# Low parts of the down projection's weights by an accumulating DMA in place of a VectorE subtraction

## The chip, the cores and the metric

The kernel runs on one core of one Trainium2 chip. The metric is the device time of one launch in microseconds (us); less is better. Several launches are timed and the median is compared. One further launch was recorded by the hardware profiler, and every row below comes from that one.

## The reference

Two decoder layers over 512 tokens of width 1024, all in float32. Each layer is RMSNorm, one combined projection, three attention branches, gates, an output projection and a residual add; then RMSNorm, a SwiGLU feed-forward part and a residual add. What matters here is the last line of each layer:

```python
h = rmsnorm(x, ln_ffn_g[l])
x = x + (jax.nn.silu(h @ w_ffn_gate[l]) * (h @ w_ffn_up[l])) @ w_ffn_down[l]
```

`w_ffn_down[l]` is 2816 by 1024. After the second layer one more RMSNorm ends the computation.

## The kernel before

**Precision by three products.** TensorE multiplies in the reduced format `float32r`. So each operand is held as two tiles, a high part (the value rounded to `float32r`) and a low part (the value less its high part), and each product is made of three matmuls into the same PSUM bank: high by high, high by low, low by high (lines 370 to 372). For a weight, the high part is a copy by ScalarE (`_hi`, line 235) and the low part is a subtraction by VectorE (`_lo`, line 243).

**Units.** Weights are loaded in units, each one tile of 128 by 1024 floats (512 KB) of the pool `wides`, which has 36 buffers (`NWIDE`). Feed-forward hidden values, norm gains and temporaries live in the same pool. Every unit has three tiles in turn: the raw load (issued on SP's queue, `_dma`), the high part and the low part. When `_lo` is written, the raw tile is given up; when the unit's matmuls are written, the high and the low part are given up (`done`).

**The down projection.** It is two jobs per layer, one for each half of the 1024 output columns (`j_dn`, lines 1429 and 1430). Each has 11 units of two 128-row blocks of the weight, so 22 units per layer and 44 in all. A unit is used by 2 blocks x 4 token blocks x 3 = 24 matmuls of 512 columns, and in each triple the second matmul is the first one that reads the low part. The second half takes its last four units in one group of eight blocks. The products' other operand, the hidden values, is split by `ffsplit` (line 1309), also one cast by ScalarE and one subtraction by VectorE for each two blocks; 4 of the 11 are written during the feed-forward stage, the others during the first half.

**What sets the order.** The order in which instructions are written is the order of each engine's queue; engines wait for one another through semaphores only. Before each token block of a unit, `ahead` (line 272) writes further loads, high parts and low parts, as far ahead as the three numbers of `look` say, in columns: `LEAN = (3072, 1024, 1024)` in the down projection means loads up to three units ahead of the current one, high parts one unit ahead, low parts one unit ahead, and at most one high and one low part per call. The feed-forward stage writes the down projection's first units near its own end: its last seven slots (one product of 12 matmuls of 256 columns each) are P1, P7, P6, P4, P5, P2, P3, and with four slots left (at P4) and two left (at P2) it calls `ahead` (line 1300), there with `NEAR`. The first of these two calls writes the high and the low part of unit 0, the second the high part of unit 1. At the end of the first half, each token block's result is added to the residual by VectorE and its sum of squares is taken by ScalarE (`residual_evac`, and `final_evac` in the second layer), in those engines' queues. From the last group of the second half, `look` is `FAR`.

In the attention part, a planner (`weave`) orders pieces of work by a modelled clock (`Clock.note`), which keeps a free time for each engine and one for the DMAs. In the down projection the order is fixed by the code above.

Of the kernel before, what the change touches and what calls it, by code (L numbers as in the profile page):

```python
# [11 lines left out]
AF = mybir.ActivationFunctionType  # L12
ALU = mybir.AluOpType
# [22 lines left out]
NEAR = (3072, 1536, 1024)  # L36
WIDE = (4096, 2048, 2048)
FAR = (6144, 4096, 4096)
LEAN = (3072, 1024, 1024)

OFF_QA, OFF_KA, OFF_VA = 0, 512, 1024
OFF_QB, OFF_KB, OFF_VB = 1536, 2048, 2560
# [125 lines left out]
class Kernel:  # L168
# [74 lines left out]
    def _lo(self, i):  # L243
        if i in self.plain:
            return
        t, cols = self.raw.pop(i)
        l = self.wide(F32R)
        self.nc.vector.tensor_tensor(l[:, :cols], t[:, :cols], self.hi[i][:, :cols], op=ALU.subtract)
        self.lo[i] = l

    def load_ahead(self, n):
# [370 lines left out]
def layer(K, l, plan, state, strip, C):  # L622
# [810 lines left out]
    def drain(jobs):  # L1433
        for _ in K.dense(jobs):
            pass

    def run():
# [62 lines left out]
        else:  # L1500
            state["g"] = K.load_g("ln_mix_g", l + 1)
        K.look = LEAN
        drain(j_dn[:1])
# [40 lines left out]
```

## Time and profile before

| | us |
|---|---|
| median of 3 launches | 1838.68 (1838.28 to 1839.81) |
| the profiled launch | 1839.35 |
| its span in the trace | 1837.6 |
| TensorE (PE) busy | 1814.9 (99%) |
| VectorE (DVE) busy | 1112.1 (61%) |
| ScalarE (ACT) busy | 883.1 (48%) |
| GpSimd (POOL) busy | 251.0 (14%) |

The granted TensorE clock was 0.997 of full speed over the span. Times in the trace count from the span's start. PE is a matmul, PEld the load of its stationary operand. A name such as `w` stands for all tiles of a pool whose names begin so (`w` is the pool of 128 by 1024 tiles, `s` that of 128 by 512 tiles, `d` and `a` are PSUM banks). All work is recorded at line 158, a helper's, so operations are told apart by tile, shape and time. A matmul's shown duration overlaps the next one's, so the pace of matmuls is read from starts, or from a long merged row divided by its count. Some records of instructions are missing from the trace.

### The profile page before, as it was taken

To read this page: it belongs to the slowest core of one execution; us is meant where nothing else is said; L and a number is where in the kernel's file an instruction comes from. 1 tells how busy PE (TensorE), PEld (TensorE's weight loads), DVE (VectorE), ACT (ScalarE), POOL (GpSimd) and SP (SyncE) were. 2 spreads that over 40 slices of the span, in tenths; PEclk is the share of its full clock that TensorE was granted. 3 is DMA by queue.
4 is the path that set the end of the run, shared out by engine and by line. 5 is a ranking of instruction groups with operands and counts; after the bars stand their busy time and mean duration, and the time that the engine had idled before them with its cause. 6 is when DMAs were issued, how large, how long until landed. Compare 5 with 4: busy or idle time off the path is not lost.

```text
span 1837.6 us, 27149 instructions
## 1 busy us (share of the span) xinstructions
PE 1814.9 (99%) x10588; PEld 1619.2 (88%) x10588; DVE 1112.1 (61%) x1832; ACT 883.1 (48%) x1701; POOL 251.0 (14%) x437
## 2 busy tenths in 40 slices
PE   7999999999999999999999999999999999999998
PEld 5999888888889999998889998888888899999886
DVE  4566556566456888773345655566664578788631
ACT  4555655554334555552235655555443355545531
POOL 3314312121000000000002252122210000000001
PEclk9999999999999999999999999999999999999999
DMA  7322122223330323242332121132252322233331
GB/s 278 117 89 72 55 72 87 100 81 131 104 138 27 112 93 107 101 149 90 134 126 95 58 69 55 60 104 86 69 178 80 115 69 93 93 115 104 126 103 46
DMA packets 63280, 183.15 MB, mean 100 GB/s; under 512 B 9296, under 2 KB 10768, under 8 KB 63152
## 3 DMA queue, kind: packets, MB, share of 16 engines
q1 hardware_dynamic: 57456, 172.84, 28.3%
q0 software_dynamic: 3824, 4.91, 0.9%
q10 hardware_dynamic: 1872, 3.67, 0.6%
q8 instruction: 83, 1.36, 0.3%
q14 instruction: 45, 0.37, 0.1%
HBM read 177.15 MB, written 8.16 MB: 101 GB/s over the span
## 4 chain that ended last, share of the span: by engine, by line
PE 94%; DVE 2%; ACT 2%; POOL 1%; issue 0%; DMA 0%; POOLq 0%; ACTq 0%
PE d L158 74%; PE a L158 21%; DVE w L158 1%; ACT w L158 1%; POOL s L158 1%; DVE s L158 0%; ACT junk L158 0%; DMA s<-in_c_onehot 0%; POOL w L158 0%; POOL m L158 0%; DVE f_A L158 0%; DVE f_S L158 0%; ACT f_A L158 0%; ACT s L158 0%; DVE h L158 0%
## 5 line engine op out<-in xcount | busy, mean ns | idle before, releaser
L158 PE MATMUL d<-w,w 128*128 128x512 f32 (+2 forms) x3888 | 748.6, 346 | 1.3 <-ACT s L158 0.9
L158 DVE TENSOR_TENSOR w<-w,w 128x1024 fp32r<-128x1024 f32 (+6 forms) x594 | 598.2, 1030 | 190.2 <-ACT w L158 161.6
L158 PEld LDWEIGHTS d<-w,w 128*128 128x128 f32 x3888 | 631.7, 190 | 83.2 <-ACT s L158 1.3
L158 PE MATMUL d<-h,w 128*128 128x512 f32 x1920 | 459.9, 392 | 0.0
L158 ACT CAST w<-w 128x1024 fp32r<-128x1024 f32 (+3 forms) x454 | 399.4, 921 | 96.2 <-PE d L158 46.9
L158 PEld LDWEIGHTS d<-h,w 128*128 128x128 f32 x1920 | 356.0, 188 | 71.4
L158 PE MATMUL d<-w,h 128*128 128x512 f32 (+2 forms) x960 | 199.0, 356 | 3.5 <-DVE h L158 1.8
L158 PEld LDWEIGHTS d<-w,h 128*128 128x128 f32 x960 | 165.1, 190 | 21.2 <-DVE h L158 2.5
L158 ACT ACTIVATE w<-w,m 128x128 f32<-128x128 f32 x192 | 107.0, 558 | 119.1 <-DVE m L158 117.8
L158 POOL TENSOR_SCALAR m<-m 128x1 f32<-128x1 f32 (+1 forms) x44 | 18.4, 419 | 1063.6 <-ACT junk L158 1063.2
L158 PE MATMUL a<-w,w 128*128 128x256 f32 (+7 forms) x912 | 157.9, 310 | 0.0
L158 PEld LDWEIGHTS a<-w,w 128*128 128x128 f32 (+1 forms) x912 | 138.3, 189 | 11.5
L158 PE MATMUL a<-f_A,w 128*128 128x256 f32 x1104 | 147.1, 283 | 0.0
L158 POOL TENSOR_SCALAR w<-w,m 128x128 f32<-128x128 f32 (+3 forms) x160 | 94.5, 608 | 352.4 <-DVE m L158 216.5
L158 PEld LDWEIGHTS a<-f_A,w 128*128 128x128 f32 x1104 | 138.7, 192 | 0.0
L158 DVE TENSOR_TENSOR w<-a,w 128x512 fp32r<-128x512 f32 (+2 forms) x162 | 90.3, 593 | 75.2 <-ACT w L158 74.7
L158 ACT CAST w<-a 128x512 fp32r<-128x512 f32 (+2 forms) x146 | 70.5, 533 | 72.5 <-PE a L158 71.8
L158 ACT ACTIVATE junk<-s 128x512 f32<-128x512 f32 (+1 forms) x40 | 23.6, 589 | 155.0 <-DVE s L158 155.0
L158 ACT COPY s<-d 128x256 f32<-128x256 f32 (+2 forms) x104 | 40.2, 391 | 108.1 <-PE d L158 107.4
L158 POOL TENSOR_SCALAR w<-w 64x512 fp32r<-64x512 f32 (+1 forms) x96 | 69.2, 728 | 125.8 <-issue 87.4
L158 PE MATMUL a<-ident,w 128*128 128x128 f32 x616 | 83.5, 275 | 2.6 <-DVE s L158 2.3
L158 DVE TENSOR_TENSOR s<-d,s 128x512 f32<-128x512 f32 x32 | 22.0, 688 | 105.4 <-PE d L158 105.4
(79 smaller groups left out, 1216.3 us busy)
## 6 DMA issues: line engine op xcount, KB each, us to landing
w<-in_weights SPq DMA_DIRECT2D x246, 512.0 KB, 3.6
w<-in_weights SPq DMA_DIRECT2D x50, 256.0 KB, 2.7
w<-in_weights SPq DMA_DIRECT2D x28, 384.0 KB, 4.3
s<-u_rep SPq DMA_DIRECT2D x24, 256.0 KB, 3.8
w<-in_weights SPq DMA_DIRECT2D x8, 288.0 KB, 3.1
w<-in_x SPq DMA_DIRECT2D x8, 256.0 KB, 7.2
s<-in_x SPq DMA_DIRECT2D x8, 256.0 KB, 5.7
x_dram<-s ACTq DMA_DIRECT2D x8, 256.0 KB, 4.2
```

What stands on the lines that cost most here:

```text
L158: return f(*args, **kw)
```

## The change

For units of the down projection's weight alone, the low part is no longer raw tile less high part on VectorE. ScalarE writes the negated high part into the low part's tile, and then a DMA issued by GpSimd adds the raw tile to it in place. The look-ahead of the down projection also changes: loads up to four units ahead in place of three, high parts three in place of one, low parts two in place of one. The calls of `ahead` at the end of the feed-forward stage are not changed.

```diff
-LEAN = (3072, 1024, 1024)
+LEAN = (4096, 3072, 2048)
...
         l = self.wide(F32R)
-        self.nc.vector.tensor_tensor(l[:, :cols], t[:, :cols], self.hi[i][:, :cols], op=ALU.subtract)
+        if self.units[i][0][0] == "w_ffn_down":
+            self.nc.scalar.activation(l[:, :cols], self.hi[i][:, :cols], AF.Copy, scale=-1.0)
+            self.nc.gpsimd.dma_start(l[:, :cols], t[:, :cols], accum_op=ALU.add)
+        else:
+            self.nc.vector.tensor_tensor(l[:, :cols], t[:, :cols], self.hi[i][:, :cols], op=ALU.subtract)
         self.lo[i] = l
```

## Rows read from the trace of the kernel before

**Rows 1.** The page's first block: busy us, share of the span, instructions.
```profile
PE 1814.9 (99%) x10588; PEld 1619.2 (88%) x10588; DVE 1112.1 (61%) x1832; ACT 883.1 (48%) x1701; POOL 251.0 (14%) x437
```

**Rows 2.** The page's chain that ended last, shares of the span by engine.
```profile
PE 94%; DVE 2%; ACT 2%; POOL 1%; issue 0%; DMA 0%; POOLq 0%; ACTq 0%
```

**Rows 3.** PE's waits, whole span: for whom, us in total, times, longest.
```profile
PE a L158 <- DMA s<-in_c_onehot: 7.9, 1, 7.9
PE a L158 <- DVE s L158: 2.3, 2, 2.0
PE d L158 <- DVE w L158: 2.0, 5, 0.5
PE d L158 <- DVE h L158: 1.8, 1, 1.8
...
PE a L158 <- DVE w L158: 0.3, 1, 0.3
```

**Rows 4.** Timeline, first layer's seam: start, us, instructions merged, [idle before <-releaser].
```profile
797.01 4.84 ACT L158 CAST w<-w 128x1024 fp32r<-128x1024 f32 x5
...
797.99 1.60 PE L158 MATMUL d<-w,w 128*128 128x256 f32 x12
798.10 2.36 DVE L158 TENSOR_TENSOR w<-w,w 128x1024 fp32r<-128x1024 f32 x2 [0.16 <-ACT w L158]
...
800.86 29.35 PE L158 MATMUL d<-w,w 128*128 128x256 f32 x134
```

**Rows 5.** Timeline of ACT alone, 798.1 to 799 us.
```profile
797.96 2.00 ACT L158 CAST w<-w 128x1024 fp32r<-128x1024 f32 x2
```

**Rows 6.** Timeline, matmuls from the first half's end on, first layer.
```profile
859.75 51.62 PE L158 MATMUL d<-w,w 128*128 128x512 f32 x227
```

**Rows 7.** Timeline of ACT, second layer's seam.
```profile
1699.90 0.84 ACT L158 ACTIVATE w<-w 128x768 f32<-128x768 f32 x1
...
1704.21 5.98 ACT L158 CAST w<-w 128x1024 fp32r<-128x1024 f32 x6
```

**Rows 8.** Timeline of PE, second layer's seam.
```profile
1708.06 67.22 PE L158 MATMUL d<-w,w 128*128 128x256 f32 x301
```

**Rows 9.** Timeline of POOL at the kernel's start: DMAs that GpSimd issued.
```profile
30.79 0.60 POOL L158 DMA_DIRECT2D cstrip<-in_c_strip  x1
```

**Rows 10.** DMA issues on the page: queue, count, KB each, median us from issue to landing.
```profile
w<-in_weights SPq DMA_DIRECT2D x246, 512.0 KB, 3.6
w<-in_weights SPq DMA_DIRECT2D x50, 256.0 KB, 2.7
```

**Rows 11.** DMA issues within 796 to 808 us.
```profile
w<-in_weights SPq DMA_DIRECT2D x6, 512.0 KB, 5.4
```

**Rows 12.** DMA issues within 829 to 858 us.
```profile
w<-in_weights SPq DMA_DIRECT2D x5, 512.0 KB, 3.4
```

**Rows 13.** DMA issues, whole span: small and queued ones of GpSimd.
```profile
cstrip<-in_c_strip POOLq DMA_DIRECT2D x1, 256.0 KB, 17.6
...
u_dram<-s POOLq DMA_DIRECT2D x2, 15.0 KB, 1.7
```

**Rows 14.** Stretches: PE, PEld, DVE, ACT, POOL busy (count), PEclk, DMA share, GB/s.
```profile
800.00:803.00 3.00, 3.00 (x24) 2.88 (x23) 2.73 (x5) 2.44 (x3) 0.00 (x0) 1.00 0.98 345
```

**Rows 15.** Timeline of ACT within the first half, first layer.
```profile
840.45 1.05 ACT L158 CAST w<-w 128x1024 fp32r<-128x1024 f32 x1 [4.16 <-PE d L158]
```

**Rows 16.** Timeline, end of the first half, first layer.
```profile
862.44 0.69 DVE L158 TENSOR_TENSOR s<-d,s 128x512 f32<-128x512 f32 x1 [0.67 <-PE d L158]
...
863.85 2.94 ACT L158 CAST w<-w 128x1024 fp32r<-128x1024 f32 x3
864.92 7.16 DVE L158 TENSOR_TENSOR w<-w,w 128x1024 fp32r<-128x1024 f32 x6 [1.79 <-ACT w L158]
...
907.50 0.30 POOL L158 TENSOR_SCALAR m<-m 128x1 f32<-128x1 f32 x1 [329.20 <-ACT junk L158]
```

**Rows 17.** Timeline, end of the first half, second layer.
```profile
1775.70 6.64 PE L158 MATMUL d<-w,w 128*128 128x512 f32 x28 [0.42 <-DVE w L158]
```

## The prediction

> **What bounds the kernel now.** I read the page's busy block first, then the chain, then PE's waits, then the timeline of the stretches in which the changed tiles are made. The busy block shows PE at 99% of the span and DVE at 61% [rows 1]; the chain that ended last is 94% PE and 2% DVE [rows 2]. So a faster DVE is worth only what PE waits for it. The list of PE's waits says how much that is: all its waits on DVE, of every kind, are 2.3 + 2.0 + 1.8 + 0.3 = 6.4 us in the whole launch, and the largest wait, 7.9 us, is for a DMA at the start [rows 3]. In the down projection PE runs without a break, but for one wait: 0.42 us for DVE in the second layer [rows 17]. The question is therefore what the new way of making a low part delays, more than what it frees.
>
> **The pace and the deadlines.** 227 matmuls of 512 columns take 51.62 us [rows 6], 0.227 us each, so a unit of 24 takes 5.46 us. In the first layer the last three products of the feed-forward stage start at 797.99 (P5), 1.435 later (P2) and at 800.86 (P3) [rows 4]; P3 ends at 802.30, and the down projection starts. Unit 0's low part is read by the second matmul, at 802.30 + 0.23 = 802.53. Unit u's is due at 802.53 + 5.46 u. In the second layer P3 starts at 1708.06 [rows 8], so all is 907.2 us later; the cast that starts at 797.01 has its like at 1704.21 [rows 7], also 907.2 later. One working serves both.
>
> **Removed.** 44 subtractions by DVE. Two of them stand in rows 4, the first one unit 0's: 2.36 us for two. All are hidden beside PE except in the place of rows 17, where unit 12's low part, written after four residual adds, comes 0.42 us late. With low parts written two units ahead, unit 12's is written ahead of those adds: gain 0.4 us, once. More than that PE can't give back here, since it waits for nothing else in the stage.
>
> **Added on ACT.** 44 negations of 128 by 1024. The trace has no such instruction; a scaled copy costs ACT what a cast does in the nearest shape, 0.84 us for 128 by 768 [rows 7], and the cast of 128 by 1024 takes 1.05 [rows 15], of which starts follow every 0.97 (4.84 / 5) [rows 4]. I take 1.05. Between 1.0 and 1.2 nothing changes: ACT then has three such instructions in a unit of 5.46 us in the first half, and two in the second.
>
> **Added on POOL and the DMA engines.** 44 DMAs. POOL has nothing else to do: its next instruction after the feed-forward stage waits until 907.5, after 329 us idle [rows 16]. The issue took it 0.60 us for a 128-partition tile [rows 9]. The landing is the unknown. From below: a plain 512 KB load that meets an idle queue lands in 3.4 us [rows 12], and 1.7 was the shortest landing of a DMA issued by GpSimd, for 15 KB [rows 13]; below 3.4 for 512 KB nothing speaks. In the stretch at issue, 800 to 803 us, the engines are 0.98 busy with weight loads at 345 GB/s [rows 14], and a load there lands in 5.4 us [rows 11]. The accumulation must read the low tile as well as the raw one. One more 256 KB costs a load 3.6 - 2.7 = 0.9 us [rows 10], so one more 512 KB read 1.8. From above: the doubled landing of a load in this stretch, 10.8; a GpSimd DMA queued behind others took 17.6 at the start [rows 13], but that one stood behind megabytes. I take 5.4 + 1.8 = 7.2 us (an estimate from these rows), nearest to the load that shares the stretch, and keep 3.4 and 10.8.
>
> **The chain at the seam, where it ends late.** The look-ahead that is widened is only that of the down projection; unit 0 is still written at P4, four slots before the end. ACT casts its high part at 797.01; the next instruction now starts at 797.96 [rows 5] and is the negation in place of a feed-forward cast; it ends at 799.0. A hop of 0.1 (DVE started 0.04 after the cast's end, 798.06 to 798.10 [rows 4]), the issue of 0.6, and 7.2 to land: 799.0 + 0.1 + 0.6 + 7.2 = 806.9. It was due at 802.53: PE stands 4.4 us. Before, DVE had it at 799.3, with 3.2 us to spare. The bounds: with 3.4 it lands at 803.1, 0.6 late; with 5.4, 2.6 late; with 10.8, 8.0 late. Two layers double each.
>
> The next units: ACT goes on with a feed-forward cast, unit 1's high part, another such cast, unit 2's high part, unit 1's negation, all 0.97 apart, so that one ends near 804.0 and lands by 811.9; due at 808.0 plus the first stall of 4.4, that is 812.4. No second stall. Unit 2's negation ends near 806 and has until 817.9. The four feed-forward casts and high parts that each move 1 us later are not due before 807.
>
> **Moved: the wider look-ahead.** Further on, each negation is written two units ahead of use. Even if ACT reached it only as that unit begins (because its buffer comes free then), cast, negation, hop and issue (1.05 + 1.05 + 0.1 + 0.6 = 2.8) would leave 10.9 - 2.8 = 8.1 us of landing within the cover. The trace shows more lead: a cast of the last units of this half is done at 841.5 [rows 15] and the second half starts at 802.30 + 60.1 = 862.4. That is 20 us. If a landing passes the cover, each us beyond it is one us of PE. The buffers: more tiles are held at once, two more high parts and one low part of 36 tiles; SP's loads queue behind those releases, and a raw tile is now held until the DMA has read it. SP is early enough by the same lead.
>
> One more place is tight. At the end of the first half ACT stands in the queue behind the sums of squares and casts again from 863.85 [rows 16]. Units up to 12 are then made; unit 14's high part and unit 13's negation follow, to 865.9; hop, issue and 7.2 give 873.8, due at 802.53 + 13 x 5.46 = 873.5. The first stall moves both sides alike, so the stall here is 0.3 in each layer (0 at 5.4, 3.9 at 10.8).
>
> **The sum.** 2 x 4.4 + 2 x 0.3 - 0.4 = +9.0 us against the profiled 1839.35 us, whose span is 1837.6. That launch is 0.67 above the median, so I forecast 1838.7 + 9.0 = 1847.7 us. The forecast's own range, landings from 5.4 to 9.0 us, is 2 x 2.6 - 0.4 = +4.8 to 2 x 6.2 + 2 x 2.1 - 0.4 = +16.2.
>
> **The rivals.**
>
> *The DMA lands in time.* For it: rows 12, since a queue's first load takes 3.4 us; then the seam costs 2 x 0.6 - 0.4 = +0.8 us, 1839.5. Up to a landing of 4.6 us the sum stays within 0.2% (2 x 1.8 - 0.4 = +3.2). Against it: rows 11 and 14, the engines are taken when it is issued. The Trainium skill, DMA: Bandwidth & Descriptors, "Anatomy of one DMA", gives for a DMA issued by GpSimd about 2.0 us plus the bytes at 436 GB/s; by that formula 512 KB would land in 3.2 us and the sum would be 2 x 0.4 - 0.4 = +0.4 us. In an idle stretch this trace agrees (3.4 for a load [rows 12]); in the stretch at issue it measures 5.4 [rows 11], and no row shows an accumulation.
>
> *The accumulation is slow and comes late twice.* At 10.8 us of landing: 2 x 8.0 + 2 x 3.9 - 0.4 = +23.4, 1862.1. If moreover one of them held the engines for longer than a unit's 5.46 us, all 44 would pace PE, 44 us for each us beyond. For it: no row has this operation. Against: a plain load of these bytes holds the engines far less, 1.8 us of its 3.6 by the difference of rows 10 (3.6 - 2.7 for a half).
>
> *Faster.* One mechanism: PE's waits on DVE go, because 44 subtractions are out of its queue. It decides if the seam costs under 0.4 us, that is a landing of up to 3.0 us, and if the waits outside the stage, 6.4 - 0.4 = 6.0 us [rows 3], go too. To pass 0.2% it needs 3.7 us of them. Against it: these waits lie in other stages, where DVE's work is not changed, and 3.0 is under every row of 512 KB. With 4 us it would be 1834.7.
>
> *The second layer's plan changes.* The planner's clock sees the added instructions and could order attention work otherwise. Against it: it decides by differences to PE's time, and between the down projection and that stage every modelled engine has waited for PE. Either sign, some 2 to 4 us.
>
> **How the numbers follow.** About 0.2% (3.7 us) is what a measurement of this kernel can tell from no change. The forecast gets 0.61, the landing in time 0.24, the slow accumulation 0.10, faster 0.03, another plan 0.02 (half of it slower). Slower by more than 0.2%: 0.61 + 0.10 + 0.01 = 0.72; within: 0.24; faster: 0.04. The range goes from 1838.3 (landing in time, and the gain of 0.4) to 1858; what lies above is the upper part of the slow case.
>
> **What would show it.** Right: the timeline has PE standing at the start of each down projection for several us, released by a DMA into a `w` tile; two long waits of PE on that DMA among PE's waits, near 802 and 1713 (the second later by the first stall); the wait of rows 17 gone; DVE's busy time lower by 44 x 1.2 = 53 us and ACT's higher by 44 x 1.05 = 46; GpSimd's DMAs landing in some 7 us in the DMA list. Wrong: no wait there and landings under 4.6 us; or waits at every unit, so that the DMAs pace the stage; or a stall of PE that is released by ACT, whose queue I hold to be early enough.

## The result and the profile after

The changed kernel takes 1864.58 us (median of 4 launches, 1862.31 to 1865.96), the kernel before 1838.51: a ratio of 1.0139 (95% interval 1.0122 to 1.0157), 26 us slower. The prediction was 1847.7 with a range up to 1858, so the sign was right and the size was not.

The busy block of the changed kernel, against [rows 1]:

```profile
span 1864.2 us, 27266 instructions
...
PE 1823.4 (98%) x10588; PEld 1624.5 (87%) x10588; DVE 1060.6 (57%) x1788; ACT 925.3 (50%) x1745; POOL 289.1 (16%) x481
```

The work moved as planned: DVE lost 51.5 us of busy time, ACT gained 42.2, POOL 38.1. But the span grew by 26.6, and PE, with the same 10588 matmuls, is busy for 8.5 us more. PE's waits in the changed kernel, against [rows 3]:

```profile
PE d L158 <- DMA w<-w: 16.6, 5, 4.2
PE a L158 <- DMA s<-in_c_onehot: 8.2, 1, 8.2
PE d L158 <- DVE w L158: 3.1, 6, 0.7
```

Five waits for the new DMAs make 16.6 us; those for DVE grew by 1.1, the one at the launch's start by 0.3. With PE's 8.5 us of longer work that is 26.5 of 26.6. PE's timeline shows the places (start, us, instructions, and what ended the idle time before them), first both ends of the first layer's down projection, then the second layer's:

```profile
801.99 1.93 PE L158 MATMUL d<-w,w 128*128 128x256 f32 x13 [0.72 <-DVE w L158]
808.14 103.22 PE L158 MATMUL d<-w,w 128*128 128x512 f32 x444 [4.23 <-DMA w<-w]
914.43 2.07 PE L158 MATMUL d<-w,w 128*128 128x512 f32 x6 [3.07 <-DMA w<-w]
918.21 8.77 PE L158 MATMUL d<-w,w 128*128 128x512 f32 x29 [1.71 <-DMA w<-w]
...
1722.94 1.93 PE L158 MATMUL d<-w,w 128*128 128x256 f32 x13 [0.72 <-DVE w L158]
1729.11 73.60 PE L158 MATMUL d<-w,w 128*128 128x512 f32 x312 [4.23 <-DMA w<-w]
1806.04 50.61 PE L158 MATMUL d<-w,w 128*128 128x512 f32 x215 [3.33 <-DMA w<-w]
```

Counting from the seam gives the units. 444 matmuls are 18 units of 24 and twelve more, which in the group of eight are the first token block of units 18 and 19: so the stalls at 914 and 918 are units 20 and 21. In the second layer 312 = 13 x 24: unit 13.

The missing 8.5 us are seen where the stretches right behind a stall are read: PE, PEld, DVE, ACT, POOL busy (count), then the granted clock, DMA share, GB/s.

```profile
804.00:808.00 4.00, 0.00 (x0) 0.00 (x0) 1.02 (x2) 4.00 (x6) 1.72 (x2) 0.78 1.08 255
808.00:810.00 2.00, 1.85 (x4) 1.49 (x5) 0.00 (x0) 1.82 (x2) 0.85 (x1) 0.50 1.06 211
810.00:812.00 2.00, 2.00 (x6) 1.59 (x5) 0.00 (x0) 0.00 (x0) 0.86 (x1) 0.50 1.07 211
812.00:814.00 2.00, 2.00 (x8) 1.54 (x8) 0.00 (x0) 0.00 (x0) 0.00 (x0) 0.73 1.03 313
...
916.00:920.00 4.00, 2.29 (x6) 1.49 (x5) 0.00 (x0) 0.00 (x0) 0.00 (x0) 0.50 0.69 230
...
1806.00:1810.00 4.00, 3.96 (x10) 3.13 (x11) 0.00 (x0) 3.90 (x4) 0.85 (x1) 0.57 1.06 270
```

After standing still, PE was granted half the clock (1.2 in place of 2.4 GHz): 6 matmuls in 2 us where the row of before has one in 0.227 us [rows 6]. The last two rows show the same behind the stalls at units 20 and 21 and, in the second layer, at unit 13.

Two lines of the page on GpSimd's DMAs: their queue (packets, MB, share of the 16 engines' time) and the new issues (count, KB each, median us from issue to landing):

```profile
q0 software_dynamic: 10160, 27.98, 7.4%
...
w<-w POOLq DMA_DIRECT2D x44, 512.0 KB, 7.9
```

An accumulation lands in 7.9 us by the median of all 44. The issue costs POOL 0.86 us (37.8 / 44) in place of 0.60 [rows 9].

### The profile page after: what moved, and what is told of

It is laid out like the page before. It is cut to its first block, busy times and chain, and to the rows that moved or that the text cites. A ratio compares the mean times of both kernels' runs of the same rounds, so it can differ in the third digit from the quotient of the medians.

```text
span 1864.2 us, 27266 instructions
## 1 busy us (share of the span) xinstructions
PE 1823.4 (98%) x10588; PEld 1624.5 (87%) x10588; DVE 1060.6 (57%) x1788; ACT 925.3 (50%) x1745; POOL 289.1 (16%) x481
## 4 chain that ended last, share of the span: by engine, by line
PE 87%; DMA 4%; issue 4%; DVE 2%; ACT 1%; POOL 1%; POOLq 0%; SPq 0%; ACTq 0%
PE d L158 67%; PE a L158 20%; DMA w<-w 3%; DVE w L158 1%; ACT w L158 1%; POOL w L158 1%; DMA w<-in_weights 1%; POOL s L158 1%; DMA s<-in_c_onehot 0%; ACT junk L158 0%; POOL m L158 0%; DVE f_A L158 0%; DVE f_S L158 0%; ACT f_A L158 0%; DVE s L158 0%
## 5 line engine op out<-in xcount | busy, mean ns | idle before, releaser
L158 PE MATMUL d<-w,w 128*128 128x512 f32 (+2 forms) x3888 | 756.9, 349 | 18.9 <-DMA w<-w 16.6
L158 DVE TENSOR_TENSOR w<-w,w 128x1024 fp32r<-128x1024 f32 (+6 forms) x550 | 546.8, 1014 | 231.4 <-ACT w L158 200.8
L158 POOL DMA_DIRECT2D w<-w x44 | 37.8, 858 | 614.8 <-ACT w L158 600.0
L158 ACT ACTIVATE w<-w 128x1024 fp32r<-128x1024 f32 (+2 forms) x80 | 73.2, 916 | 68.6 <-DVE w L158 48.7
```

The costliest lines, as they stand in the source:

```text
L158: return f(*args, **kw)
```

## The experiments

All are timed against the kernel before on the same chip, where it had medians of 1838.1 to 1839.7. Differences to the changed kernel use its 1864.6, which comes from four launches beside 1838.5 of before.

**1. The look-ahead alone.**

```diff
 (kernel before)
-LEAN = (3072, 1024, 1024)
+LEAN = (4096, 3072, 2048)
```

> The kernel before with the wider look-ahead alone (LEAN = 4096, 3072, 2048) and VectorE's subtractions kept. Theory A (the loss comes from the DMA's late landing): as before, 1838.5 us, or 0.4 less, because unit 12's low part in the second layer is then written ahead of the residual adds (the 0.42 us wait of PE goes). Rival B (the wider look-ahead holds so many buffers that ACT and SP fall behind): slower than before by a good part of the 26 us, 1845 or more, with PE waits in the second half of the down projection.

Measured: 1838.11 us, ratio 0.9999 (0.9990 to 1.0009). The wait of [rows 17] is gone: PE's matmuls into `d` banks wait 1.3 us in all for DVE's `w` tiles, in place of 2.0 [rows 3]. The gain is too small to be measured, and the look-ahead alone is not the cause of the loss. Rival B falls.

**2. The DMA alone.**

```diff
 (changed kernel)
-LEAN = (4096, 3072, 2048)
+LEAN = (3072, 1024, 1024)
```

> The DMA alone: the changed kernel with the old look-ahead. Theory A: the seam stall of 4.2 us per layer stays; at the end of the first half the unit whose negation stands behind the sums of squares is now unit 12, due 5.5 us earlier than unit 13, so it lands some 6 to 8 us late in each layer (negation ends near 866, issue and 7.9 us of landing make 874.8, due 868), and the clock falls after it: some 8 to 16 us above the changed kernel, 1873 to 1880 us. Rival B (buffers): faster than the changed kernel, as fewer tiles are held. Rival C (the DMA engines pace the stage): the same as the changed kernel, 1864.6, as the same bytes are moved.

Measured: 1870.27 us, ratio 1.018 (1.0165 to 1.0196), 5.7 above the changed kernel. The sign is theory A's, the size below its 8 to 16. PE's waits for the DMAs did grow by 8.0 us (24.6 against 16.6), but PE's busy time, 1819.5 us, is 3.9 below the changed kernel's: the slower matmuls behind the stalls cost less in this launch, though it has more stalls. PE's timeline has the place that was named, unit 12 (288 = 12 x 24 matmuls behind the seam), in both layers:

```profile
808.01 67.80 PE L158 MATMUL d<-w,w 128*128 128x512 f32 x288 [5.21 <-DMA w<-w]
879.45 35.65 PE L158 MATMUL d<-w,w 128*128 128x512 f32 x156 [3.64 <-DMA w<-w]
...
1729.51 67.81 PE L158 MATMUL d<-w,w 128*128 128x512 f32 x288 [5.44 <-DMA w<-w]
1805.04 56.54 PE L158 MATMUL d<-w,w 128*128 128x512 f32 x239 [7.72 <-DMA w<-w]
```

The wider look-ahead thus does its part for unit 12, and the stall moves one unit on only in the second layer. The second row also shows that not every stall is followed by slower matmuls: behind 3.64 us of waiting the 156 take 0.229 us each, at a granted clock of 1.00. The seams' waits are 5.21 and 5.44 us here, where 4.2 was expected to stay.

**3. The first three units by VectorE.**

```diff
 (changed kernel; `at` is the unit's number in the layer's down projection)
-        if self.units[i][0][0] == "w_ffn_down":
+        name, _, k, c0 = self.units[i][0]
+        at = k // 2 + 11 * (int(c0[0]) // 512)
+        if name == "w_ffn_down" and at not in (0, 1, 2):
```

> The changed kernel, but the low parts of units 0, 1 and 2 of each layer's down projection by VectorE's subtraction as before. Theory A (the seam stalls because unit 0 is written four slots ahead and its DMA lands late; the half clock and the 0.72 us wait of P3 follow from it): the 4.23 and 0.72 us waits go in both layers and so does the half clock behind them (2.2 and 2.6 us): 9.9 + 4.9 = 14.8 us less than the changed kernel, 1849.8. Rival D (matmuls run slower because of the DMAs' traffic, not because of the stall): only the waits go, 9.9 us less, 1854.7, and matmuls after the seam keep a lower pace. The waits at units 20 and 21 of the first layer and 13 of the second stay in both.

Measured: 1848.40 us, ratio 1.0059 (1.0042 to 1.0077), 16.2 less than the changed kernel; expected were 14.8 (A) or 9.9 (D). The four launches lie between 1845.2 and 1852.0, still clear of rival D's 1854.7. The profiled one is the slowest, with a span 13.9 us below the changed kernel's. Both seams are without a wait, and what is left are three waits for the DMAs at the later places:

```profile
PE d L158 <- DMA w<-w: 6.6, 3, 2.8
```

A seam thus costs some 7 to 8 us per layer (half of 13.9 to 16.2), of which only 4.2 are the wait that was predicted.

**4. PE kept busy through the seam's stall.**

```diff
 (changed kernel, in n_job's body, ahead of the first matmul)
+if wname == "w_ffn_down" and cols[0] == 0 and kb == 0 and tb == 0:
+    for _ in range(19):
+        self.tc.nc.tensor.matmul(o, ah, h, start=True, stop=True)
 mm(o, ah, h, start=kb == 0, stop=False)
```

> The changed kernel with 19 more matmuls at the start of each down projection, into the bank that the first real matmul then overwrites: high by high of unit 0, which needs no low part, 19 x 0.227 = 4.3 us of PE work that fill the seam's stall. Theory A (the clock is halved because PE stands still): PE no longer stands, the granted clock stays at full, and the two seams give back 2.2 + 2.6 = 4.8 us: 1859.8 us. Rival D (the slow matmuls behind the seam come from the DMA traffic): the low part still lands at the same time and the matmuls behind it are as slow as before: 1864.6 us.

Measured: 1861.08 us, ratio 1.0127 (1.0110 to 1.0144): 3.5 less than the changed kernel with 38 matmuls more. The same stretch as above, of this kernel:

```profile
804.00:808.00 4.00, 2.87 (x13) 2.06 (x11) 0.00 (x0) 3.47 (x4) 1.70 (x2) 1.00 1.08 232
808.00:810.00 2.00, 1.95 (x8) 1.61 (x9) 0.00 (x0) 1.15 (x2) 0.56 (x1) 1.00 1.02 201
810.00:812.00 2.00, 2.00 (x10) 1.68 (x9) 0.00 (x0) 0.00 (x0) 0.30 (x1) 1.00 1.08 223
```

The DMA engines are as full as in the changed kernel (1.02 to 1.08), but the granted clock stays at 1.00, and PE does 10 matmuls in 2 us where the changed kernel does 6. So the slow matmuls come from PE's standing still, not from the DMAs' traffic; rival D falls. The gain is 1.3 below the expected 4.8, and 1.19 us of the first seam's wait was left.

**5. The DMA as a plain copy.**

```diff
 (changed kernel; the addition is left out)
-self.nc.gpsimd.dma_start(l[:, :cols], t[:, :cols], accum_op=ALU.add)
+self.nc.gpsimd.dma_start(l[:, :cols], t[:, :cols])
```

> The changed kernel with the DMA copying the raw tile over the low part's tile in place of adding it (the addition is left out, so the low parts are the full weights). Theory A (the accumulation costs the DMA engines more than a copy, because it also reads its destination): the landing of a lone one falls from 4.5 us towards the 3.4 of a plain load, that of the seam's first one from 8.4 to about 6, GpSimd's queue takes some 4% of the engines' time in place of 6.5%, and the seam's stall falls from 4.2 us to about 2. Rival E (the landing is the price of a DMA issued by GpSimd, whatever it does): landings, share and stall stay.

One launch: 1853.72 us. The queue's share and the landing, to be read against the changed kernel's 7.4% and 7.9 us:

```profile
q0 software_dynamic: 10160, 27.98, 4.3%
...
w<-w POOLq DMA_DIRECT2D x44, 512.0 KB, 3.8
```

Before, this queue held 0.9% of 1837.6 us for other transfers, 16.5 us. A copy therefore holds the 16 engines for (4.3% x 1852.0 - 16.5) / 44 = 1.4 us, an accumulation for (7.4% x 1864.2 - 16.5) / 44 = 2.8 us: twice as long for the same 512 KB. In the issue lists of single short stretches, accumulations that met little other traffic landed in 4.5 us (issued at 841.6 and 856.2), copies in 2.9 (840.9 and 847.5). So rival E falls and theory A's mechanism holds, but not its size at the seam: the first copy there still took 7.3 us where the first accumulation took 8.4, and the waits are 3.08 and 3.32, not the 2 that was expected. For the first DMA at the seam the sharing with the weight loads weighs more (7.3 less 2.9 is 4.4 us) than the addition (8.4 less 7.3 is 1.1). By the formula of the Trainium skill, DMA: Bandwidth & Descriptors, "Anatomy of one DMA", 512 KB would take 3.2 us, an estimate; the copy in a quiet stretch agrees with it (2.9), an accumulation there does not (4.5), and at the seam neither does (7.3 and 8.4).

**6. The next layer's loads one token block later.**

```diff
 (changed kernel)
             if i == 27:
+                K.look = (0, 0, 0)
+            if i == 29:
                 K.look = FAR
```

> The changed kernel, but the loads for the next layer that the last group of the second half writes at its start are written one token block later. Theory A (units 20 and 21 come late in the first layer because their DMAs share the engines with those loads: landings of 9.4 and 12.2 us where a lone one takes 4.5): both are in time, the waits of 3.07 and 1.71 us and the half clock behind them (about 2.9 us) go, 7.7 us less than the changed kernel, 1856.9. Rival B (their negations are late on ACT because ACT waits for buffers that earlier DMAs hold; GpSimd issues them at 904 to 906 for use at 912): at most 2 us less.

Measured: 1857.89 us, ratio 1.0108 (1.0091 to 1.0125), 6.7 less than the changed kernel (A: 7.7, B: at most 2). The waits at units 20 and 21 are gone:

```profile
806.83 111.56 PE L158 MATMUL d<-w,w 128*128 128x512 f32 x479 [4.60 <-DMA w<-w]
...
1720.66 72.47 PE L158 MATMUL d<-w,w 128*128 128x512 f32 x312 [4.40 <-DMA w<-w]
1796.20 51.88 PE L158 MATMUL d<-w,w 128*128 128x512 f32 x215 [3.06 <-DMA w<-w]
```

The first of these rows runs on through the group of eight. GpSimd issued units 20 and 21 at 901.9 to 903.7, against 904.2 to 906.0 in the changed kernel. But PE is 1.3 us earlier too (806.83 against 808.14), so the lead grew by 1.0 us only: the edit holds back not just the next layer's loads but also its first cast, which ACT did ahead of the two negations. Unit 20's landing fell from 10.2 us to 5.6, and the median of the two from 11.6 to 7.1. So most of the gain is the landing.

**7. The first units written earlier.**

```diff
 (changed kernel)
-            if rest in (6, 4, 2):
+            if rest in (16, 13, 10, 7):
+                K.look = LEAN
                 K.ahead(job.base + 2 * NG - 1, 1)
```

> The changed kernel, all 44 DMAs kept, but the down projection's first units are written from 13 slots before the end of the feed-forward stage (at 16, 13, 10 and 7 slots left, with the down projection's look-ahead) in place of 4. Theory A (the seam's price is one of lead only): the stalls at both seams and their half clock go, 8.5 + 4.8 = 13.3 us less than the changed kernel, 1851.3, up to 1.4 us less still if P3's wait goes too. Rival F (the DMA is not hidden wherever it stands, it fills engines that the feed-forward stage's loads need): another wait takes its place in the feed-forward stage, and less than half of this is gained.

Measured: 1852.05 us, ratio 1.0069 (1.0054 to 1.0084), 12.5 less than the changed kernel (A: 13.3). Of the three old calls the first, at 6, writes no part of these units; the other two are those at P4 and P2. With the new ones neither seam waits for a DMA. PE waits 1.2 us more for ACT in the feed-forward stage, 0.63 in each layer, since negations now stand among the copies that free its banks.

**8. The tight units by VectorE, the others by the DMA.**

```diff
 (as experiment 3)
+        if name == "w_ffn_down" and at not in (0, 1, 2, 13, 20, 21):
```

> The changed kernel, but the low parts of units 0, 1, 2, 13, 20 and 21 of each layer (12 of 44) by VectorE; the other 32 by the DMA. Theory A (each place of loss is one whose low part lands late; the other DMAs are hidden): the time of before, 1838.5 us, to within 1.5. Rival D (the DMAs' traffic slows matmuls or pushes other work at large): a part in proportion stays, 5 us or more above before.

Measured: 1838.25 us, ratio 0.9998 (0.9989 to 1.0008). 32 DMAs remain, and they cost nothing that can be measured. One stretch with them, of this kernel and then of the kernel before:

```profile
830.00:860.00 30.00, 30.00 (x134) 24.86 (x133) 4.37 (x4) 10.23 (x11) 3.47 (x4) 1.00 0.67 156
...
830.00:860.00 30.00, 30.00 (x134) 24.82 (x134) 5.51 (x6) 3.88 (x5) 0.00 (x0) 1.00 0.28 88
```

Both do 134 matmuls in these 30 us, at a DMA share of 0.67 and of 0.28; between 870 and 900 us it is 134 again, at 1.00 and 0.47. Traffic as such did not slow PE.

**9. All 44 by the DMA, with three moves.** Experiments 6 and 7 together, and the look-ahead one unit longer:

```diff
-LEAN = (4096, 3072, 2048)
+LEAN = (5120, 4096, 3072)
```

> All 44 low parts by the DMA, with three moves and no subtraction brought back: the first units written from 13 slots before the seam (as in x7_early), the next layer's loads one token block later (as in x6_far_late), and a look-ahead one unit longer (5120, 4096, 3072), so that unit 13 is written ahead of the sums of squares of the second layer. Theory A (only lateness costs, and each place has its own lead): the three remaining places of loss of x7_early go too (2.8 + 2.2 us and 3.5 us and the half clock behind them), and the time is that of before to within 2 us, 1838 to 1841. Rival B (longer holds leave too few buffers): the wait at unit 13 or another one stays, 1845 or more.

Measured: 1845.85 us, ratio 1.0042 (1.0030 to 1.0054): a miss of theory A's 1838 to 1841 by 4.9 us, and the time that rival B named (1845 or more). PE waits for no DMA any more, but for ACT:

```profile
795.77 1.70 PE L158 MATMUL d<-w,w 128*128 128x256 f32 x12 [1.72 <-ACT s L158]
...
1707.12 1.88 PE L158 MATMUL d<-w,w 128*128 128x256 f32 x12 [2.98 <-ACT s L158]
```

ACT's timeline of the second layer shows why (the last lines are the copies that PE waits for):

```profile
1705.75 1.06 ACT L158 ACTIVATE w<-w 128x1024 fp32r<-128x1024 f32 x1 [1.35 <-DMA w<-w]
1706.71 0.35 ACT L158 COPY s<-d 128x256 f32<-128x256 f32 x1
1706.96 0.38 ACT L158 COPY s<-a 128x256 f32<-128x256 f32 x1
```

The longer look-ahead, used in the feed-forward stage too, wrote one negation more there, and in the second layer it had to wait for a tile that an earlier accumulation still held. That is rival B's reason.

**10. Unit 0 alone by VectorE.**

```diff
 (as experiment 3)
+        if name == "w_ffn_down" and at not in (0,):
```

> The changed kernel, but the low part of unit 0 alone by VectorE in each layer. Theory A (each of the first units has its own deadline, and unit 1 is only hidden behind unit 0's stall): unit 1's negation ends one slot of ACT earlier, near 803.2, its DMA lands some 7 us later, near 810.5, due near 808.2: a stall of about 2.3 us in place of 4.2, P3's wait of 0.72 gone, two layers: 5.3 us less than the changed kernel and some of the half clock, 1856 to 1859. Rival G (unit 0 is the only late one): as with the first three by VectorE, 1848.4.

Measured: 1859.36 us, ratio 1.0113 (1.0100 to 1.0126), 0.4 above theory A's 1856 to 1859 and far from rival G. Unit 1 stalls in place of unit 0, for 4.09 and 3.38 us where 2.3 was expected.

**11. As experiment 9, the early calls with the shorter look-ahead.**

```diff
 (kernel of experiment 9)
-                K.look = LEAN
+                K.look = (4096, 3072, 2048)
                 K.ahead(job.base + 2 * NG - 1, 1)
```

> As x9_all, but the four early calls in the feed-forward stage keep the shorter look-ahead (4096, 3072, 2048), so that unit 2 is not written there; the longer one (5120, 4096, 3072) holds from the down projection's start. In x9_all no wait of PE for a DMA was left, but ACT stood 1.35 us for a tile that a DMA held, with the copies that free the banks of the feed-forward products queued behind it: PE waited 3.0 us there in the second layer, at half clock after it, and 1.7 us in the first. Theory A (the rest of x9_all is that wait): PE's waits on ACT fall to about 2.1 us in all, as in x7_early, none on a DMA: 1839 to 1841 us. Rival H (44 negations and DMAs cost some 7 us wherever they stand): 1845 again, with another wait in its place.

Measured: 1839.48 us beside 1839.70 of before on that chip, ratio 1.0003 (0.9994 to 1.0012). PE's waits of this kernel, and the start of its busy block:

```profile
PE a L158 <- DMA s<-in_c_onehot: 8.1, 1, 8.1
PE a L158 <- DVE s L158: 2.3, 2, 2.1
PE d L158 <- ACT s L158: 2.2, 4, 0.6
PE d L158 <- DVE h L158: 1.8, 1, 1.8
PE d L158 <- DVE w L158: 1.7, 4, 0.6
...
PE 1813.5 (99%) x10588; PEld 1618.2 (88%) x10588; DVE 1060.8 (58%) x1788; ACT 926.2 (50%) x1745; POOL 289.6 (16%) x481
```

All 44 accumulations are hidden and the whole 26 us are back. So are the 8.5 us of PE's longer work: with all 44 DMAs but without the stalls PE is busy for 1813.5 us, against 1814.9 before [rows 1]. Nothing is gained over before either; PE's one wait in this stage, 0.42 us, was all there was to gain. No version beats both kernels beyond what the measurement can tell.

## Why the prediction was wrong

**What held.** That PE bounds the kernel and DVE's 44 subtractions free nothing that can be measured; that PE stands several us at each seam and a DMA into a `w` tile releases it, 4.4 us predicted, 4.23 measured; that the wider look-ahead takes away the wait at unit 12 (experiment 1). Experiments 3 and 7 show the seam's cause: with the subtraction back, or with more lead, it goes. The timeline of the seam reads as the prediction's chain does:

```profile
797.26 1.05 ACT L158 CAST w<-w 128x1024 fp32r<-128x1024 f32 x1
...
798.35 1.06 ACT L158 ACTIVATE w<-w 128x1024 fp32r<-128x1024 f32 x1
...
799.71 1.00 POOL L158 DMA_DIRECT2D w<-w  x1 [221.15 <-ACT w L158]
800.38 1.23 DVE L158 TENSOR_TENSOR w<-w,w 128x1024 fp32r<-128x1024 f32 x1 [2.19 <-ACT w L158]
801.52 0.42 DVE L158 TENSOR_TENSOR w<-d,s 128x256 f32<-128x256 f32 x1
```

**That the seam's stall came out so near is in part luck.** Counted from unit 0's cast (797.26 here, 797.01 in [rows 4]), the low part landed 10.9 us later and not 9.9 as the chain had it: the landing took 8.4 us, and the issue began late. (A landing counts from the start of the issue: 799.71 + 8.4 = 808.1, where PE goes on. The chain's 0.6 + 7.2 counted the issue twice.) But P3 started 0.9 us later as well (4.73 us after the cast, against 3.85), for a reason that the prediction did not have, told below. The two misses cancel. The negation's 1.05 us was right too, but not by its row: the ACTIVATE of 128 by 768 in [rows 7] is the feed-forward part's SiLU, not a scaled copy.

**The step that failed first: a stall was priced at its length.** The sum has 2 x 4.4 us for the seams and nothing for what follows. PE's half clock behind the stalls added 8.5 us, the largest missing term. Experiment 4 shows that it hangs on PE's standing still, and experiment 11 that it goes with the stalls.

**The cover of two units did not hold in the group of eight.** The sum has nothing for units 20 and 21. The cover of 10.9 us counted two whole units. In the last group one token block runs through four units, so unit 20 is due 12 matmuls, 2.7 us, after unit 18 begins, and unit 21 1.4 us later. There the next layer's loads start as well. In the changed kernel GpSimd's two issues at 904 to 906 us have a median landing of 11.6 us. Waits of 3.07 + 1.71 us follow; experiment 6 takes them away by moving the loads.

**"One working serves both" did not hold at unit 13.** It was given 0.3 us in each layer; measured were 0 in the first and 3.33 in the second. In the second layer the first half's evacuation also multiplies by the final norm's gain on DVE, between the adds. The sums of squares on ACT, first and last of four, first layer and then second:

```profile
867.02 0.63 ACT L158 ACTIVATE junk<-s 128x512 f32<-128x512 f32 x1 [6.69 <-DVE s L158]
...
871.16 0.63 ACT L158 ACTIVATE junk<-s 128x512 f32<-128x512 f32 x1 [0.64 <-DVE s L158]
...
1788.29 0.63 ACT L158 ACTIVATE junk<-s 128x512 f32<-128x512 f32 x1 [6.53 <-DVE s L158]
...
1794.71 0.63 ACT L158 ACTIVATE junk<-s 128x512 f32<-128x512 f32 x1 [1.42 <-DVE s L158]
```

They follow each other by 1.38 us in the first layer and by 2.14 in the second, so unit 13's negation behind them starts 3 x 0.76 = 2.3 us later. Its DMA also took longer to land, 8.4 us (issued at 1797.63) against 5.3 (874.07): in the second layer weight loads were issued beside it.

**P3's wait was not seen.** The prediction let the feed-forward casts move 1 us later "not due before 807". Due they were not, but behind the cast's subtraction on DVE (800.38, after 2.19 us of idle time) stands the add that frees P3's bank (801.52): P3 waits 0.72 us in each layer. Experiment 3 has it gone with the negation.

**The near hit of a rival is no credit.** The slow accumulation was priced at 1862.1 us, by landings of 10.8 everywhere and 8.0 at each seam. The measured time is close to it for other reasons: landings of 7.9, 4.2 at each seam, and the clock.

What stays open: why the seams waited 4.4 to 4.6 us in experiment 6 and 5.2 to 5.4 in experiment 2, not 4.2; and why the slower matmuls cost PE so differently from run to run, 8.5 us more busy time than before at 16.6 us of waits for the DMAs, 4.6 at 24.6 (experiment 2, where one stall of 3.64 us left the clock as it was), 1.4 at 9.1 (experiment 5).

## What to carry to other kernels

Work moved off an engine that is not the bound brought nothing here; what counted is the lead of each tile over its first use, and it is to be checked at every place where the order of use changes (a seam between stages, evacuations in the queue, a group that runs through several tiles at once), in each layer by itself. A stall of PE is to be priced with the slower matmuls behind it, here 8.5 us on 16.6, and as a range, since other runs paid less. When the lead can't be had, keep the fast path for the few tight tiles: 12 of 44 were enough here.

## What the runs showed of the hardware that was not expected

A DMA that adds to its destination in SBUF held the 16 engines for 2.8 us per 512 KB, a copy for 1.4, and GpSimd took 0.86 us to issue the one and 0.53 the other. Accumulations beside matmuls left the pace of PE as it was: 134 matmuls in 30 us at a DMA share of 0.28 without them and of 0.67 with them (experiment 8). Stalls of PE of 3.1 to 4.2 us amid dense matmuls were followed by a granted clock of 0.50 to 0.57 in the changed kernel, one of 3.64 us in experiment 2 was not, and 19 matmuls whose result is overwritten, put into the stall at each seam, kept it at 1.00 (experiment 4).
